# A two-layer encoder trunk on one core: the third part of each feed-forward's down product by seven products, and four last outputs by halves of the tokens

## The chip, the cores and the metric

The kernel runs on one core of one Trainium2 chip. The metric is the device time of one execution in microseconds (us); lower is better. The engines are named as the profile names them: PE is the matrix engine, DVE the vector engine, ACT the scalar engine, POOL and SP the two that issue most DMAs here.

## The reference

512 tokens of width 1024 go through two layers. Each layer is: a SwiGLU feed-forward (inner width 2816), a mixer (layer 0: windowed attention beside a recurrent block; layer 1: gated DeltaNet), a second feed-forward, and a gate that mixes in a per-layer embedding `p`. After the first three parts comes a residual and a layer norm. All is float32.

```python
def swiglu(x, wg, wu, wd):
    return (jax.nn.silu(x @ wg) * (x @ wu)) @ wd

for i in range(DEPTH):
    x = layer_norm(DN_ALPHA * x + 0.5 * swiglu(x, ffn1_wg[i], ffn1_wu[i], ffn1_wd[i]), ln_g[i, 0], ln_b[i, 0])
    y = mixer_ab(x, ...) if i % 2 == 0 else mixer_c(x, ...)
    x = layer_norm(DN_ALPHA * x + y, ln_g[i, 1], ln_b[i, 1])
    x = layer_norm(DN_ALPHA * x + 0.5 * swiglu(x, ffn2_wg[i], ffn2_wu[i], ffn2_wd[i]), ln_g[i, 2], ln_b[i, 2])
    x = x + jax.nn.sigmoid(x @ ple_wg[i] + ple_bg[i]) * (p[i] @ ple_wp[i])
```

## The kernel before, in words

**Layout.** Activations lie feature by token: `xf[0..7]` are eight tiles of 128 features by 512 tokens. A weight tile is 128 by 128. The width 1024 makes `KD = 8` tiles, the inner width 2816 makes `MF = 22` inner tiles.

**Precision.** Every product is done as three matmuls of a shorter float format: a number is split into a high part (a cast on ACT) and a low part (a subtraction on DVE), and `mm3` (line 466) multiplies low by high, high by high and high by low. So each weight tile and each activation tile costs ACT and DVE a cast and a subtraction before PE can use it. The weights' splits are issued by `splitter`, which runs ahead of PE by `self.ahead` steps (`AHEADS = 5` steps inside the feed-forward, `AHEADF = 10` at its end); a step is four weight tiles side by side, 128 by 512, in the plain way.

**Seven products for eight.** `block` multiplies a two by two arrangement (two output tiles by two halves of the tokens, over pairs of input tiles) with seven products in place of eight (`PRODUCTS`). It needs sums and differences of the weights (`s1` to `s4`, made by DVE once and otherwise by DMAs that add in flight, `addload`), differences of the activations (`diffs`, `hforms` for the inner tiles), copies of partial results (`snap`, on ACT) and additions when results are taken out (`done`). Its matmuls are 256 tokens wide.

**A feed-forward** (`ffn`) has the order of `FFN_ORDER`: inner tiles 0 to 6 up, then tiles 0 to 5 down by seven products, tiles 7 to 12 up, tiles 6 to 11 down by seven products, tiles 13 to 21 up, and last tiles 12 to 21 down in the plain way. A `down` block over three pairs of inner tiles has 7 x 3 x 3 = 63 matmuls, there are four of them for eight outputs, and their results are added onto `xf`. Inner tiles that go down by seven products are prepared by `hforms`, the others only split (`self.hs`).

**The feed-forward's end** (`ffn_ln`) does the plain part, output after output over the ten inner tiles that are left, and the layer norm. `first` takes output 0, makes a mean over its features on PE and subtracts it from all eight `xf` (DVE, eight operations 128 by 512). `take` adds an output onto `xf[m]`, squares it (ACT), and adds it and its square onto two running sums (DVE). The last two outputs are done by halves of the tokens: first half of both, then second half of both. When all outputs of a half are taken, `tail` sums over features on PE, makes the norm's factors on DVE and ACT, and spawns eight `apply`, one per feature tile: three DVE and two ACT operations, 128 by 256, that end in the split tile the next stage reads. The next stage starts with a group of four outputs by halves of the tokens (`group(..., halves=True)`): 8 x 12 matmuls of the first half, then as many of the second. After a layer's second feed-forward three small outputs of `p` (`ple_p`, 18 matmuls 512 wide) stand ahead of that group.

**What sets the order.** Each engine executes in the order in which the program issues instructions. The program issues PE's matmuls one after another and weaves the other engines' work between them by times that it estimates (`tick`, `due_at`); on the chip only the order and the waits on data are left. Eight PSUM banks are handed on in turn.

Of the kernel before, what the change touches and what calls it, by code (L numbers as in the profile page):

```python
# [29 lines left out]
KD = D // P  # L30
MF = DFF // P
# [7 lines left out]
HT = T // 2  # L39
TA, TB = slice(0, HT), slice(HT, T)  # L40

FFN_ORDER = (("up", 0, 7), ("down", 0, 6), ("up", 7, 13), ("down", 6, 12), ("up", 13, MF),
             ("plain", 12, MF))
NPLAIN = 3


def stream_plan():


    def ffn():  # L50
        o = [("P", NPLAIN * 2 * KD)]
        for what, a, b in FFN_ORDER:
            if what == "up":
# [169 lines left out]
class Kern:  # L223
# [388 lines left out]
    def y(self, k, cs):  # L612
        self.until(lambda: self.ys[k] is not None)
        return self.ys[k]

    def ffn(self, i, n, l):
# [8 lines left out]
        self.hs = [None] * MF  # L625
        j0 = FFN_ORDER[-1][1]

# [103 lines left out]
        self.ahead = AHEADS  # L731
        for what, a, b in FFN_ORDER:
            if what == "up":
# [9 lines left out]
    def ffn_ln(self, i, l, desc, y, nk):  # L743

        S, V, G, PE = self.S.l, self.V.l, self.G.l, self.PE.l
        self.__dict__.pop("x", None)
        xf = self.xf
        st = {"taken": [0, 0], "c": False}

        def first(p_):  # L750
            yield V.scalar_tensor_tensor(xf[0], p_, 0.5, xf[0], ALU.mult, ALU.add)
            self.psfree(self.V)
            hi, lo = yield from self.split(xf[0])
            pc = yield from self.bank(0)
            yield [PE.matmul(pc, self.ones128, hi.bitcast(F32R), start=True, stop=False),
                   PE.matmul(pc, self.ones128, lo.bitcast(F32R), start=False, stop=True)]
            st["q"], st["s"] = self.tl(), self.tl()
            for m in range(KD):
                yield V.tensor_tensor(xf[m], xf[m], pc, ALU.subtract)
            self.psfree(self.V)  # L760
            yield S.activation(st["q"], xf[0], AF.Square)
            st["c"] = True

        def take(m, p_, cs, free, add):
            while not st["c"]:
                yield None
            yield V.scalar_tensor_tensor(xf[m][:, cs], p_[:, cs], 0.5, xf[m][:, cs], ALU.mult, ALU.add)
            if free:
                self.psfree(self.V)
            sq = self.tl()  # L770
            yield S.activation(sq[:, cs], xf[m][:, cs], AF.Square)
            a, s, q = xf[m][:, cs], st["s"][:, cs], st["q"][:, cs]
            yield add.l.tensor_tensor(s, xf[0][:, cs] if m == 1 else s, a, ALU.add)
            yield add.l.tensor_tensor(q, q, sq[:, cs], ALU.add)
            for half in range(2):
                if cs == FULL or cs == HALVES[half]:
                    st["taken"][half] += 1

        for m in range(KD - 2):
            if m == KD - 4:  # L780
                self.ahead = AHEADF
            p_ = self.mtile(desc(m), y, nk)
            self.spawn(first(p_) if m == 0 else take(m, p_, FULL, True, self.V), 1)
        self.S.activation(self.tiny(1), self.epsln, AF.Abs_reciprocal_sqrt)
        if l != 1:
            self.spawn(self.load_p(i), 2)
        self.xh, self.xl = [None] * KD, [None] * KD
        self.napply = [0, 0]
        ps, ws = {}, {}
        st["p"] = [self.ps() for _ in range(2)]  # L790
        for half, cs in enumerate(HALVES):
            for m in (KD - 2, KD - 1):
                if half == 0:
                    ps[m] = self.ps()
                for k in range(nk):
                    if half == 0:
                        ws[m, k] = self.w(desc(m)(k))
                    yh, yl = y(k, cs)
                    self.mm3(ps[m][:, cs], ws[m, k], yh[:, cs], yl[:, cs], k == 0, k == nk - 1)
                self.spawn(take(m, ps[m], cs, half == 1, self.V), 1)  # L800
            self.spawn(self.tail(i, l, half, cs, st), 1)
        self.ahead = 6
        self.xdone, self.xs = lambda k: self.napply[1] > k, lambda k: (self.xh[k], self.xl[k])
# [910 lines left out]
```

## Time and profile before

| what | value |
|---|---|
| median of 2 runs | 2029.3 us (2028.8 to 2029.8) |
| the profiled execution's own time | 2027.8 us |
| its span in the profile | 2026.1 us |
| mean granted clock of PE | 0.996 |
| PE busy, DVE busy, ACT busy | 98%, 80%, 61% |
| moved by DMA | 273.69 MB, mean 135 GB/s |

The span is what the profile covers; the execution's own time has 1.7 us more around it. A busy PE in the profile is not a PE at its peak, since matmuls overlap, so durations of stretches of matmuls are worked out from the distance between starts. The same holds for DVE and ACT: an operation's length in the timeline overlaps the next one's start, and the distance from start to start is what it takes from the engine.

### The profile page before, as it was taken

How to read it: one execution, taken by the hardware profiler on the slowest of the kernel's cores; microseconds unless marked ns; L12 is line 12 of the kernel's file. 1: busy time of each engine (PE TensorE's matmuls, PEld its weight loads, DVE VectorE, ACT ScalarE, POOL GpSimd, SP SyncE). 2: the span in 40 equal slices, each digit the busy share in tenths (PEclk: the TensorE clock that was granted, in tenths of full speed). 3: DMA queues.
4: the chain of work that ended last, by engine and by line, in shares of the span. 5: the costliest groups of instructions: out<-in, count | busy, mean ns of one | idle time of the engine just before them, and what ended most of it. 6: DMA issues, size and time to landing. Idle time of an engine off the chain costs nothing.

```text
span 2026.1 us, 39662 instructions
## 1 busy us (share of the span) xinstructions
PE 1991.8 (98%) x15237; PEld 1844.4 (91%) x15237; DVE 1621.3 (80%) x3360; ACT 1235.4 (61%) x2841; POOL 322.5 (16%) x372
## 2 busy tenths in 40 slices
PE   8999999999999999999999999999999999999999
PEld 7999998878899999898999998987877989999988
DVE  8888777779998887788888777887776898887676
ACT  5666664796766666465666664685644566666554
POOL 1223210000023232000232210021100013232100
PEclk9999999999999999999999999999999999999999
DMA  7787975123358798424797974131221257888631
GB/s 228 153 195 163 201 170 177 32 64 103 92 122 199 155 208 181 138 82 108 145 205 155 207 172 146 44 101 53 52 80 54 66 122 165 186 178 191 164 102 42
DMA packets 105053, 273.69 MB, mean 135 GB/s; under 512 B 11792, under 2 KB 25248, under 8 KB 104864
## 3 DMA queue, kind: packets, MB, share of 16 engines
q1 hardware_dynamic: 57024, 188.81, 29.8%
q0 software_dynamic: 47840, 82.35, 26.1%
q8 instruction: 120, 1.97, 0.4%
q14 instruction: 69, 0.57, 0.1%
HBM read 269.00 MB, written 2.11 MB: 134 GB/s over the span
## 4 chain that ended last, share of the span: by engine, by line
PE 76%; DVE 16%; ACT 5%; DMA 2%; issue 2%; SPq 0%; POOL 0%; DVEq 0%; ACTq 0%; POOLq 0%
PE ps L162 76%; DVE t L162 15%; ACT t L162 4%; DMA wr<-w 1%; DMA t<-w 1%; ACT L162 0%; SPq L1499 0%; DVE y L162 0%; POOL y L162 0%; POOL t L433 0%; DVEq L162 0%; DVE der L162 0%; ACTq L162 0%; ACT y L162 0%; DVE o L162 0%
## 5 line engine op out<-in xcount | busy, mean ns | idle before, releaser
L162 PE MATMUL ps<-t,t 128*128 128x256 f32 (+4 forms) x14824 | 1964.5, 296 | 30.0 <-DVE t L162 19.9
L162 PEld LDWEIGHTS ps<-t,t 128*128 128x128 f32 (+2 forms) x14824 | 1798.5, 184 | 167.1 <-DVE t L162 40.0
L162 DVE TENSOR_TENSOR t<-t,t 128x512 fp32r<-128x512 f32 (+4 forms) x870 | 477.5, 574 | 89.3 <-ACT t L162 79.4
L162 DVE TENSOR_TENSOR t<-wr,t 128x512 fp32r<-128x512 f32 (+2 forms) x729 | 463.2, 659 | 19.8 <-ACT t L162 13.7
L162 ACT CAST t<-t 128x512 fp32r<-128x512 f32 (+2 forms) x697 | 357.0, 537 | 172.7 <-DVE t L162 159.7
L162 ACT CAST t<-wr 128x512 fp32r<-128x512 f32 (+2 forms) x729 | 402.4, 598 | 2.6 <-DMA wr<-w 2.6
L162 ACT COPY t<-ps 128x256 f32<-128x256 f32 (+1 forms) x475 | 184.1, 389 | 252.6 <-PE ps L162 249.1
L433 POOL DMA_DIRECT2D wr<-w x108 | 93.2, 863 | 1046.0 <-DVE t L162 749.6
L162 DVE SCALAR_TENSOR_TENSOR t<-t,t 128x256 f32<-128x256 f32 (+1 forms) x348 | 177.1, 515 | 75.3 <-ACT t L162 68.4
L433 POOL DMA_DIRECT2D t<-w x216 | 191.3, 1000 | 137.7 <-DVE t L162 51.3
L162 ACT ACTIVATE t<-t 128x256 f32<-128x256 f32 (+1 forms) x190 | 93.6, 500 | 182.7 <-DVE t L162 179.4
L162 DVE SCALAR_TENSOR_TENSOR t<-ps,t 128x256 f32<-128x256 f32 (+2 forms) x174 | 84.5, 489 | 67.2 <-PE ps L162 66.6
L162 DVE TENSOR_TENSOR t<-t 128x256 f32<-128x256 f32 x212 | 89.2, 421 | 57.9 <-ACT t L162 54.5
L162 ACT ACTIVATE t<-ps 128x128 f32<-128x128 f32 (+2 forms) x204 | 70.8, 358 | 88.4 <-PE ps L162 86.9
L162 DVE TENSOR_TENSOR t<-ps,t 128x256 f32<-128x256 f32 (+2 forms) x188 | 81.8, 435 | 13.9 <-PE ps L162 10.1
L162 DVE SCALAR_TENSOR_TENSOR t<-ps,vec,t 128x511 f32<-128x511 f32 (+3 forms) x92 | 68.3, 746 | 20.6 <-ACT t L162 16.4
L162 DVE TENSOR_TENSOR t<-wr,wr 128x512 f32<-128x512 f32 (+1 forms) x108 | 69.6, 644 | 1.9 <-DMA wr<-w 1.9
L162 ACT ACTIVATE t<-t,vec,der 128x256 f32<-128x256 f32 x96 | 56.0, 597 | 4.5 <-DVE t L162 4.5
L162 ACT ACT_TABLE_LOAD x37 | 47.5, 1283 | 11.1 <-DVE t L162 8.5
L162 POOL TENSOR_TENSOR y<-y,sm 128x8 f32<-128x8 f32 (+1 forms) x16 | 22.7, 1420 | 188.2 <-DVE y L162 188.2
L162 DVE SCALAR_TENSOR_TENSOR t<-t,der,t 128x256 f32<-128x256 f32 x96 | 45.7, 477 | 0.0
L162 DVE TENSOR_TENSOR t<-t,ps 128x512 f32<-128x512 f32 (+1 forms) x62 | 33.3, 578 | 7.3 <-PE ps L162 5.6
(69 smaller groups left out, 438.1 us busy)
## 6 DMA issues: line engine op xcount, KB each, us to landing
wr<-w SPq DMA_DIRECT2D x296, 512.0 KB, 4.3
t<-w POOLq DMA_DIRECT2D x152, 256.0 KB, 5.9
wr<-w SPq DMA_DIRECT2D x66, 384.0 KB, 3.6
wr<-w POOLq DMA_DIRECT2D x76, 256.0 KB, 4.8
t<-w POOLq DMA_DIRECT2D x64, 192.0 KB, 4.8
wr<-w POOLq DMA_DIRECT2D x32, 192.0 KB, 4.3
t<-x SPq DMA_DIRECT2D x8, 256.0 KB, 6.1
t<-p SPq DMA_DIRECT2D x8, 256.0 KB, 4.9
```

Of the source, the lines that this page charges most:

```text
L162: getattr(self.e, op.name)(*op.a, **op.kw)
L433: self.nc.gpsimd.dma_start(t, src, accum_op=ALU.add)
```

## The change

Tiles 12 to 17 go down by seven products too, ahead of the last three up tiles; only tiles 18 to 21 go down in the plain way. At the end four outputs, not two, are done by halves of the tokens. `self.ahead` goes to 10 at the first plain output, not at the fifth.

```diff
-FFN_ORDER = (("up", 0, 7), ("down", 0, 6), ("up", 7, 13), ("down", 6, 12), ("up", 13, MF),
-             ("plain", 12, MF))
+FFN_ORDER = (("up", 0, 7), ("down", 0, 6), ("up", 7, 13), ("down", 6, 12), ("up", 13, 19), ("down", 12, 18),
+             ("up", 19, MF), ("plain", 18, MF))
+
+NHALF = 4
...
-        for m in range(KD - 2):
-            if m == KD - 4:
+        for m in range(KD - NHALF):
+            if m == 0:
                 self.ahead = AHEADF
...
-            for m in (KD - 2, KD - 1):
+            for m in range(KD - NHALF, KD):
```

In the whole program PE gets 912 more matmuls 256 wide and 528 fewer 512 wide. DVE gets 244 more operations 256 wide, 128 more 384 wide and 72 fewer 512 wide. POOL issues 48 more DMAs that add in flight.

The first place is DVE at the end of the first feed-forward of layer 0, where the last outputs are taken (`t_80` to `t_87` are `xf[0]` to `xf[7]`, `wr` are raw weights, `ps` are PSUM banks). Before, output 6 and output 7 of the first half:

```order
L162 SCALAR_TENSOR_TENSOR t_86<-ps_4563,t_86 128x256
L162 TENSOR_TENSOR t_4621<-wr_4461,t_4620 128x512
L162 TENSOR_TENSOR t_4300<-t_4300,t_86 128x256
L162 TENSOR_TENSOR t_4299<-t_4299,t_4616 128x256
L162 TENSOR_TENSOR t_4640<-wr_4461,t_4639 128x512
L162 TENSOR_TENSOR t_4570<-t_4567,t_4569 128x512
L162 TENSOR_TENSOR t_4664<-wr_4476,t_4663 128x512
L162 SCALAR_TENSOR_TENSOR t_87<-ps_4613,t_87 128x256
L162 TENSOR_TENSOR t_4300<-t_4300,t_87 128x256
L162 TENSOR_TENSOR t_4299<-t_4299,t_4673 128x256
L162 TENSOR_TENSOR t_4684<-t_4300,t_4684 128x256
```

After, output 3 whole, then outputs 4 to 7 of the first half:

```order
L164 SCALAR_TENSOR_TENSOR t_83<-ps_4829,t_83 128x512
L164 SCALAR_TENSOR_TENSOR t_84<-ps_4853,t_84 128x256
L164 SCALAR_TENSOR_TENSOR t_85<-ps_4875,t_85 128x256
L164 TENSOR_TENSOR t_4808<-t_4808,t_83 128x512
L164 TENSOR_TENSOR t_4807<-t_4807,t_4898 128x512
L164 TENSOR_TENSOR t_4808<-t_4808,t_84 128x256
L164 TENSOR_TENSOR t_4807<-t_4807,t_4905 128x256
L164 TENSOR_TENSOR t_4808<-t_4808,t_85 128x256
L164 TENSOR_TENSOR t_4807<-t_4807,t_4911 128x256
L164 SCALAR_TENSOR_TENSOR t_86<-ps_4891,t_86 128x256
L164 SCALAR_TENSOR_TENSOR t_87<-ps_4908,t_87 128x256
L164 TENSOR_TENSOR t_4808<-t_4808,t_86 128x256
```

The weight splits between the outputs are gone, and four outputs of the first half are taken one behind the other.

The second place is DVE a little later, where the first half is normalised (`der` holds the norm's gains). Before, from output 3's first operation on:

```order
L162 SCALAR_TENSOR_TENSOR t_4774<-t_83,der,t_4710 128x256
L162 TENSOR_TENSOR t_4844<-ps_4562,t_4844 128x256
L162 TENSOR_TENSOR t_4749<-t_82,t_4748 128x256
L162 TENSOR_TENSOR t_83<-t_4774 128x256
L162 SCALAR_TENSOR_TENSOR t_4824<-t_84,der,t_4710 128x256
L162 SCALAR_TENSOR_TENSOR t_4844<-t_4844 128x256
L162 SCALAR_TENSOR_TENSOR t_4845<-t_4844,t_4845 128x256
L162 TENSOR_TENSOR t_4845<-ps_4561,t_4845 128x256
L162 TENSOR_TENSOR t_4776<-t_83,t_4775 128x256
L162 TENSOR_TENSOR t_84<-t_4824 128x256
L162 SCALAR_TENSOR_TENSOR t_4851<-t_85,der,t_4710 128x256
L162 TENSOR_TENSOR t_4826<-t_84,t_4825 128x256
```

After, from output 2's last operation to output 4's first:

```order
L164 TENSOR_TENSOR t_5054<-t_82,t_5053 128x256
L164 TENSOR_TENSOR t_4813<-wr_4669,t_4812 128x512
L164 TENSOR_TENSOR t_5135<-wr_4669,t_5134 128x512
L164 TENSOR_TENSOR t_5142<-wr_4703,t_5141 128x512
L164 TENSOR_TENSOR t_5151<-wr_4703,t_5150 128x512
L164 TENSOR_TENSOR t_5162<-wr_4744,t_5161 128x512
L164 TENSOR_TENSOR t_5166<-wr_4744,t_5165 128x512
L164 TENSOR_TENSOR t_5078<-t_5075,t_5077 128x512
L164 SCALAR_TENSOR_TENSOR t_5063<-t_83,der,t_5010 128x256
L164 TENSOR_TENSOR t_83<-t_5063 128x256
L164 SCALAR_TENSOR_TENSOR t_5106<-t_84,der,t_5010 128x256
```

Six weight splits, and one of `p`, now stand between output 2 and output 3; before, the norm of outputs 3 to 5 ran through with no split between.

## Rows read from the trace of the kernel before

**Rows 1.** The page, part 1: busy time, share of the span, instructions.
```profile
PE 1991.8 (98%) x15237; PEld 1844.4 (91%) x15237; DVE 1621.3 (80%) x3360; ACT 1235.4 (61%) x2841; POOL 322.5 (16%) x372
```

**Rows 2.** Windows of the first feed-forward; columns: window, length, busy (instructions), clock, DMA, GB/s.
```profile
120.00:180.00 60.00, 58.70 (x483) 57.89 (x482) 48.16 (x96) 39.33 (x91) 15.57 (x18) 1.00 0.77 164
180.00:220.00 40.00, 39.90 (x330) 39.42 (x329) 34.40 (x73) 24.21 (x57) 13.04 (x15) 1.00 0.92 205
240.00:300.00 60.00, 60.00 (x502) 60.00 (x501) 42.61 (x75) 37.46 (x83) 11.29 (x13) 1.00 0.78 177
301.00:357.00 56.00, 56.00 (x307) 48.85 (x306) 40.31 (x71) 25.32 (x48) 4.32 (x8) 1.00 0.53 169
```

**Rows 3.** Timeline, DVE, first feed-forward's end; start, length, engine, line, operation, tiles, idle, releaser.
```profile
301.72 0.69 DVE L162 SCALAR_TENSOR_TENSOR t<-t,t 128x512 f32<-128x512 f32 x1 [0.74 <-ACT t L162]
...
303.10 0.69 DVE L162 TENSOR_TENSOR t<-t,t 128x512 fp32r<-128x512 f32 x1
...
311.09 4.87 DVE L162 TENSOR_TENSOR t<-t,ps 128x512 f32<-128x512 f32 x8 [0.28 <-PE ps L162]
...
322.21 0.69 DVE L162 SCALAR_TENSOR_TENSOR t<-ps,t 128x512 f32<-128x512 f32 x1 [2.05 <-PE ps L162]
...
329.01 0.69 DVE L162 SCALAR_TENSOR_TENSOR t<-ps,t 128x512 f32<-128x512 f32 x1 [2.91 <-PE ps L162]
...
350.29 1.77 DVE L162 TENSOR_TENSOR t<-t,t 128x256 f32<-128x256 f32 x4
...
356.80 0.42 DVE L162 TENSOR_TENSOR t<-t 128x256 f32<-128x256 f32 x1
```

**Rows 4.** The same timeline, later: 256-wide operations back to back.
```profile
377.96 0.42 DVE L162 TENSOR_TENSOR t<-t 128x256 f32<-128x256 f32 x1
378.30 0.47 DVE L162 SCALAR_TENSOR_TENSOR t<-t,der,t 128x256 f32<-128x256 f32 x1
```

**Rows 5.** Timeline, DVE, stretch 180 to 220: 384-wide weight splits.
```profile
195.73 1.49 DVE L162 TENSOR_TENSOR t<-wr,t 128x384 fp32r<-128x384 f32 x3
```

**Rows 6.** Timeline, PE, first feed-forward's end.
```profile
357.71 1.95 PE L162 MATMUL ps<-t,t 128*128 128x256 f32 x12 [0.29 <-ACT t L162]
...
360.28 0.39 PE L162 MATMUL ps<-t,o 128*128 128x256 f32 x1 [0.18 <-DVE t L162]
...
365.39 18.98 PE L162 MATMUL ps<-t,t 128*128 128x256 f32 x155 [0.67 <-DVE t L162]
```

**Rows 7.** Timeline, PE, second feed-forward's end.
```profile
874.27 7.56 PE L162 MATMUL ps<-t,t 128*128 128x256 f32 x49
...
883.77 21.51 PE L162 MATMUL ps<-t,t 128*128 128x256 f32 x178
```

**Rows 8.** Timeline, PE, second stretch of inner tiles and what follows.
```profile
122.79 13.21 PE L162 MATMUL ps<-t,t 128*128 128x256 f32 x108 [0.31 <-ACT t L162]
136.35 20.42 PE L162 MATMUL ps<-t,t 128*128 128x256 f32 x168 [0.36 <-DVE t L162]
...
177.82 72.45 PE L162 MATMUL ps<-t,t 128*128 128x256 f32 x595 [0.28 <-DVE t L162]
```

**Rows 9.** Timeline, PE, end of layer 0's mixer.
```profile
539.27 7.58 PE L162 MATMUL ps<-t,t 128*128 128x256 f32 x48 [2.13 <-DVE t L162]
```

**Rows 10.** Windows of 2 us, end of layer 0's mixer.
```profile
540.00:542.00 2.00, 2.00 (x12) 2.00 (x11) 1.84 (x6) 1.50 (x4) 0.00 (x0) 0.51 0.97 242
542.00:544.00 2.00, 2.00 (x14) 2.00 (x13) 1.01 (x3) 0.73 (x2) 0.00 (x0) 0.64 0.90 304
```

**Rows 11.** Timeline, PE, end of layer 1's mixer.
```profile
1632.59 28.29 PE L162 MATMUL ps<-t,t 128*128 128x256 f32 x165 [1.72 <-ACT t L162]
```

**Rows 12.** Windows of 2 us, end of layer 1's mixer.
```profile
1632.00:1634.00 2.00, 1.38 (x4) 1.09 (x5) 1.90 (x6) 1.82 (x4) 0.00 (x0) 0.57 0.68 162
1634.00:1636.00 2.00, 2.00 (x11) 2.00 (x11) 1.58 (x5) 1.02 (x3) 0.00 (x0) 0.50 1.09 320
...
1638.00:1640.00 2.00, 2.00 (x15) 2.00 (x14) 2.00 (x5) 1.30 (x4) 1.71 (x3) 0.72 0.38 44
```

## The prediction

> **What bounds the kernel now.** I read the page's busy shares first, then windows by stage, then the timelines of PE and DVE at the places that the change touches. PE is busy for 98% of the span and its weight loads for 91%, DVE for 80% [rows 1]. The windows show that this 80% is no even load: DVE has 48.2 of 60 us in the second stretch of inner tiles, 34.4 of 40 in the second down part, 42.6 of 60 in the third stretch and 40.3 of 56 in the plain part at the end [rows 2]. So PE sets the pace, and the plain part is where DVE has room: it waits 2 to 3 us for each output [rows 3]. The change takes matmuls away from PE and puts more DVE work next to the one place where PE waits for DVE by construction, the layer norm.
>
> **Paces.** From start to start, a 256-wide matmul takes 0.120 us (502 in 60 us [rows 2]); a 512-wide one 0.227 us (30 matmuls between two outputs taken at 322.21 and 329.01, 6.80 us [rows 3]). DVE takes 0.60 for a 512-wide operation (eight in 4.87, less the overlap of the last [rows 3]), 0.34 for a 256-wide one (377.96 to 378.30 [rows 4]), about 0.40 with the norm's gains, by their length [rows 4], and 0.47 for a 384-wide one [rows 5].
>
> **Term 1, PE's work.** Per feed-forward, before: six outputs whole, 6 x 30 x 0.227 = 40.8 us, and two by halves, 120 x 0.120 = 14.4, together 55.2. After: 252 matmuls of seven products, 30.2; four outputs whole, 48 x 0.227 = 10.9; four by halves, 96 x 0.120 = 11.5; together 52.6. That is -2.6 per feed-forward, -10.3 us for four. The saving is small because a 512-wide matmul costs less than two 256-wide ones: one product in eight is saved, and 6% of that width's speed is given back.
>
> **Term 2, the third part's inner tiles.** Tiles 12 to 17 now need differences and splits of activations, as tiles 6 to 11 do. In that stretch PE waits 0.31, 0.36, 0.36 and 0.28 us, once at the start and once per pair of tiles [rows 8]; in the third stretch it waits for nothing (60.00 of 60 [rows 2]). I take the same 1.3 us for the new pairs: +5.2 us in all. Ends: 0, if the waits fall into slack, and 8. The weights' sums come by 12 more adding DMAs per feed-forward on POOL's queue and by raw tiles of 384 KB on SP's; the second down part runs with the DMA engines 92% busy and PE busy for 39.9 of 40 us [rows 2], so I cost them at nothing. If that cover were gone, a late sum would hold a block, and the term's upper end allows for it.
>
> **Term 3, the end of a feed-forward that a mixer follows (two of four).** Zero is PE's first plain matmul; in the trace of before DVE's last operation for the last inner tile starts 0.5 us behind it, at 301.72. From there to the operation that ends output 0 of the first half, the changed order has 57 DVE rows without a break for PE: 28 that are 512 wide (the splits of the last weights and of four steps of the mixer's, the eight subtractions, four whole outputs), 28 that are 256 wide (four half outputs three times over, two of the second half, the statistics) and one with gains. 28 x 0.60 + 28 x 0.34 + 0.40 = 26.7 us, so the last of them starts at 26.9, and the first product follows 0.9 later (356.80 to 357.71 in before [rows 3, 6]): 27.8. PE's own work to there is 10.9 + 11.5, two 512-wide matmuls for the mean and four 256-wide statistics, 0.9, and 0.4 for the last inner tile's split, which now is wanted at the tenth plain matmul (2.0 us) and not the twenty-eighth: 23.7. So PE waits 4.1 us. Then the eight groups of twelve, 11.5 us plus 0.5 of statistics, are paced by DVE: the next 40 rows (24 that are 256 wide, 9 that are 512 wide, 7 with gains) take 16.4 us, and because six weight splits and one of `p`, 4.2 us, stand between output 2 and output 3, the fourth group can start at about 38.8 and the eighth ends at 46.3. That is 6.5 us more of waiting. Total, with the 0.4, 11.0, against 0.29 + 0.18 + 0.67 = 1.2 in before [rows 6]: +9.8 each, +19.6 us. Ends: +4 each if the splits slip behind the group or DVE overlaps better, +14 each if ACT, which casts for each of these splits, is late too.
>
> **Term 4, the end that a gate follows (the other two).** The same 57 rows stand on DVE, but 18 matmuls of `p`, 4.1 us, stand on PE ahead of the group: 23.7 + 4.1 = 27.8, so the first wait is covered. The first three groups then wait 2.4 us for DVE's statistics of the second half; with the 0.4 above 2.8 us, where before PE ran through [rows 7]. +5.6 us in all; ends 0 and +12, since weight splits stand between the outputs of the second half as well.
>
> **Term 5, PE's clock.** No run here shows PE idle 4 us at this place. The nearest rows are the mixers' ends: after 2.13 us of idling the granted clock is 0.51 and 0.64 of full for 2 us each, 1.7 us lost [rows 9, 10]; after 1.72 us idle it is 0.57, 0.50, 0.50 and 0.72, 3.4 us lost [rows 11, 12], where the window left out reads like the one before it. I take 2.6, the mean, for each mixer-side end: +5.2 us. Ends: 0, if slow groups only fill the wait for DVE, and 5.8 each, half speed for four groups.
>
> **Sum.** -10.3 + 5.2 + 19.6 + 5.6 + 5.2 = +25.3 us. The profiled execution took 2027.8 us (span 2026.1 and 1.7 around it); the median is 1.5 above that. So 2029.3 + 25.3, about 2054 us. With all terms at their low ends it is -10 + 8 = 2027; with all at their high ends, -10 + 8 + 28 + 12 + 12 = +50, 2079. Two per cent of the time before is 40.6 us, about what a measurement of this kernel can tell from no change: 1988.7 and 2069.9 are the bounds, and the forecast is a small loss within them.
>
> **Rivals.** *A, PE stays the only bound.* If the ends of the feed-forwards keep their cover, only terms 1 and, in part, 2 are left: -10.3 to -5, 2019 to 2024, not slower than before. Its place is the norm of the first half, its price the 57 rows; it decides if DVE needs under 23 us for them. For it: DVE is idle 28% of the plain part now [rows 2]. Against it: that part shrinks from 55 to 23 us of PE's work, and the mean's eight subtractions and eight outputs' takings stay. The Trainium skill, Perfetto Trace Analysis, section Identifying the Most-Contended Engine, judges TensorE by its weight-load share and the others by occupancy and has one optimise the highest first; by that rule this change is right, and it would give A's time. The trace agrees with the ranking (91% to 80%) but its windows show that the ranking turns over at the norm, so I give A little.
>
> *B, the clock stays down through the whole group.* The gaps between groups of twelve come again and again, each a chance to lose the clock; at 0.5, the lower of its two levels, eight groups take 23.0 us, not 11.5. Two such ends cost 2 x 11.5 where I took 2 x 2.6: +18, 2072. It decides if the granted clock is 0.5 until the group's second half. For it: the 1.72 us gap cost 6 us of low clock [rows 11, 12]. Against it: groups five to eight come without a gap, and the waits of 0.18 and 0.67 us in before left the clock whole. [...]
>
> **Chances.** The forecast 0.72, with 2036 to 2068 as its own range; A 0.13; B 0.15. The range that is to hold the time eight times in ten leaves out most of A and the far end of B: 2027 to 2076. Slower by over 2%: most of B and a little of the forecast's upper end, 0.12. Faster by over 2% would need 40 us where PE's work shrinks by 10: 0.01. Within 2%: 0.87.
>
> **What would show it.** In the changed profile: PE's busy time down by about 8 to 10 us plus what a low clock adds; PE rows at the first and third feed-forwards' ends with waits for DVE of about 4 us before the first group and 4 before the fourth; waits of 0.3 to 0.4 us per pair of tiles in the third stretch; a granted clock under 1 right behind the first and third feed-forward; DVE near 10 tenths there. It would be wrong if the waits at those ends stay near 1 us (then A), if the clock is low for over 6 us there (then B), or if PE waits for weights in the third down part, which nothing above prices.

## The result and the profile after

The kernel after takes 2091.55 us (median; 2091.33 to 2091.77), before 2029.3. The ratio is 1.0311, with a 95% interval of 1.0294 to 1.0328: 62 us slower, where the forecast was 25 us and its range ended at 2076. The prediction was wrong.

The page of after, part 1, which answers to [rows 1]:

```profile
PE 2009.8 (96%) x15621; PEld 1869.1 (89%) x15621; DVE 1719.6 (82%) x3660; ACT 1293.3 (62%) x3012; POOL 364.4 (17%) x420
```

PE's busy time rose by 18 us although it has less work, and its share fell by two points: the granted clock was 0.982 over the span, not 0.996, and PE waited more. The view of waits says for whom (us in total, times, longest). Before:

```profile
PE ps L162 <- DVE t L162: 20.3, 38, 3.7
PE ps L162 <- ACT t L162: 9.3, 10, 4.2
```

After:

```profile
PE ps L164 <- ACT t L164: 44.1, 21, 4.6
PE ps L164 <- DVE t L164: 31.4, 65, 3.4
```

The sum goes from 29.6 to 75.5 us. Where these waits stand is seen by marks. Each layer norm makes a mean over the features by a pair of 512-wide matmuls with the tile of ones, `ps<-t,o`, and these rows cut the PE timeline into stages (first feed-forward and mixer of layer 0, then of layer 1). Before:

```profile
310.43 0.62 PE L162 MATMUL ps<-t,o 128*128 128x512 f32 x2
...
493.53 0.62 PE L162 MATMUL ps<-t,o 128*128 128x512 f32 x2
...
1226.16 0.62 PE L162 MATMUL ps<-t,o 128*128 128x512 f32 x2
...
1586.37 0.62 PE L162 MATMUL ps<-t,o 128*128 128x512 f32 x2
```

After:

```profile
339.77 0.62 PE L164 MATMUL ps<-t,o 128*128 128x512 f32 x2
...
505.84 0.62 PE L164 MATMUL ps<-t,o 128*128 128x512 f32 x2
...
1281.07 0.62 PE L164 MATMUL ps<-t,o 128*128 128x512 f32 x2
...
1637.04 0.64 PE L164 MATMUL ps<-t,o 128*128 128x512 f32 x2
```

The first difference, 29.3 us, is the third part, which now stands ahead of the mean; the same 29.3 is taken from the stage that ends at 1281.07 and given to the next one, so that each place holds one whole feed-forward. For each other kernel below, its own first difference is used. So, in us over before:

| kernel | first feed-forward, layer 0 | second, layer 0 | first of layer 1, with its mixer | second, layer 1 | span |
|---|---|---|---|---|---|
| predicted | +11.1 | +1.5 | +11.1 | +1.5 | +25 |
| after | +12.3 | +13.3 | +25.1 | +12.8 | +63.5 |
| tiles only | +9.3 | +18.3 | +25.2 | +15.5 | +68.3 |
| halves only | -2.5 | +1.1 | +14.0 | +0.6 | +13.2 |
| banks | +11.2 | +14.8 | +13.2 | +15.0 | +54.1 |
| p, first try | +11.0 | +13.3 | +25.1 | +10.5 | +59.8 |
| p up | +8.4 | +7.7 | +23.7 | +7.2 | +47.1 |
| no mean | +2.4 | +8.9 | +18.4 | +6.6 | +36.2 |
| banks, p, look-ahead | +10.2 | +6.4 | +10.1 | +11.2 | +37.9 |
| the same, no mean | +3.3 | +1.0 | +4.1 | +2.2 | +10.6 |
| halves, all reliefs, no mean | -1.5 | +5.7 | +1.9 | +3.1 | +9.2 |
| halves and banks | -3.0 | +0.3 | -0.9 | +0.7 | -2.9 |
| before, no mean | -2.1 | +3.0 | -2.0 | +0.6 | -0.5 |

Each row is one execution. The last one, of a kernel that takes as long as before, shows how far the places move by themselves: up to 3 us, so smaller differences are not read here.

The first column came near the forecast. The second and fourth missed by some 12 us each, and the third by 14, of which layer 0's column says that about 13 lie in the mixer. These three places are the 37 us that the forecast lacked.

**The first feed-forward's end** has the waits that the prediction walked to. PE's timeline there, against [rows 6]:

```profile
361.74 2.43 PE L164 MATMUL ps<-t,t 128*128 128x256 f32 x9 [4.37 <-ACT t L164]
...
374.53 20.70 PE L164 MATMUL ps<-t,t 128*128 128x256 f32 x146 [3.13 <-ACT t L164]
```

There is a wait of 4.37 ahead of the first group and one of 3.13 ahead of the fourth. ACT is named because it casts last, but the view of DVE shows who is late, against [rows 3]:

```profile
340.49 4.87 DVE L164 TENSOR_TENSOR t<-t,ps 128x512 f32<-128x512 f32 x8
345.27 1.29 DVE L164 SCALAR_TENSOR_TENSOR t<-ps,t 128x512 f32<-128x512 f32 x2
...
368.81 3.69 DVE L164 TENSOR_TENSOR t<-wr,t 128x512 fp32r<-128x512 f32 x6
372.43 0.68 DVE L164 TENSOR_TENSOR t<-t,t 128x512 fp32r<-128x512 f32 x1
```

The idle of 2 to 3 us ahead of each output is gone: the outputs are ready before DVE is. The six weight splits and the one of `p` stand where the order of instructions had them, and the fourth group waits behind them. Windows of 2 us there (columns as in [rows 2]):

```profile
368.00:370.00 2.00, 2.00 (x11) 2.00 (x11) 1.97 (x5) 2.00 (x5) 0.00 (x0) 0.50 0.00 0
...
376.00:378.00 2.00, 2.00 (x11) 2.00 (x11) 1.90 (x7) 1.98 (x5) 0.00 (x0) 0.50 0.13 51
...
380.00:382.00 2.00, 2.00 (x16) 2.00 (x16) 1.82 (x6) 1.23 (x4) 0.00 (x0) 0.82 0.00 0
382.00:384.00 2.00, 2.00 (x19) 2.00 (x18) 1.90 (x6) 1.65 (x4) 0.00 (x0) 1.00 0.04 8
```

The clock is 0.50, the lower of its two levels (1.2 and 2.4 GHz), behind each of the two waits, with 11 matmuls per window and not 19, and it is whole again from about 381 on.

**The second feed-forward's end**, where [rows 7] show no wait at all:

```profile
895.78 0.39 PE L164 MATMUL ps<-t,o 128*128 128x256 f32 x1 [4.57 <-ACT t L164]
896.35 0.58 PE L164 MATMUL ps<-t,o 128*128 128x256 f32 x1 [0.18 <-DVE t L164]
...
902.84 32.53 PE L164 MATMUL ps<-t,t 128*128 128x512 f32 x225 [4.58 <-ACT t L164]
```

That is 9.3 us of waiting where 2.8 was forecast. What waits is told by the order of PE's instructions there (`t2298` and `t2299` are high and low part of `p`'s first tile, `t2332` and `t2333` of its second, `t2330` and `t2334` the second half's running sums, `o2` the ones):

```
L164 MATMUL ps2315_11919<-t2298_11761,t2273_11670 128x512
L164 MATMUL ps2315_11919<-t2298_11761,t2272_11669 128x512
L164 MATMUL ps2294_11755<-t2330_11952,o2_116 128x256 [waits Activation_49]
L164 MATMUL ps2294_11755<-t2330_11952,o2_116 128x256 [waits DVE_49]
L164 MATMUL ps2315_11919<-t2299_11762,t2272_11669 128x512 [waits DVE_49]
L164 MATMUL ps2295_11756<-t2334_11966,o2_116 128x256 [waits Activation_49]
L164 MATMUL ps2295_11756<-t2334_11966,o2_116 128x256 [waits DVE_49]
L164 MATMUL ps2315_11919<-t2332_11958,t2273_11670 128x512 [waits Activation_49]
```

After two matmuls of `p` PE stands at the second half's statistics, which DVE adds up only between the norm's operations of the first half (4.57 us), and then at the second tile of `p`, whose cast and subtraction stand behind the casts of four normalised tiles (4.58). The other 15 matmuls of `p` queue behind both. Both loads of `p` are issued long before, at 874.4 and 874.9, and by the profile take about 5 us to land, so it is the place of the splits on ACT and DVE and not the load that is late. The clock falls here too; from 896 to 906 the windows show 0.50 to 0.53:

```profile
904.00:906.00 2.00, 2.00 (x6) 1.57 (x6) 1.54 (x5) 1.38 (x3) 0.00 (x0) 0.50 0.00 0
```

**The end of layer 1's mixer** has no instruction that the change touches. Before, the serial chains of heads 6 and 7 (DeltaNet steps, 128 wide, each waiting on the last) ran at the same time; now they run one after the other, and PE waits for the end of the second:

```profile
1628.03 1.12 PE L164 MATMUL ps<-cst,t 128*128 128x128 f32 x4 [3.38 <-DVE t L164]
```

The end of each chain is seen on POOL, which takes the power of its norm. Before, the two lie 4 us apart:

```profile
1567.84 1.01 POOL L162 TENSOR_TENSOR y<-y,sm 128x4 f32<-128x4 f32 x1 [44.46 <-DVE y L162]
1572.02 1.01 POOL L162 TENSOR_TENSOR y<-y,sm 128x4 f32<-128x4 f32 x1 [3.17 <-DVE y L162]
```

and after 17:

```profile
1609.36 1.36 POOL L164 TENSOR_TENSOR y<-y,sm 128x4 f32<-128x4 f32 x1 [38.01 <-DVE y L164]
1626.05 1.01 POOL L164 TENSOR_TENSOR y<-y,sm 128x4 f32<-128x4 f32 x1 [15.33 <-DVE y L164]
```

### The profile page after: what moved, and what is told of

It is laid out like the page before. It is cut to its first block, busy times and chain, and to the rows that moved or that the text cites. A ratio compares the mean times of both kernels' runs of the same rounds, so it can differ in the third digit from the quotient of the medians.

```text
span 2089.6 us, 41202 instructions
## 1 busy us (share of the span) xinstructions
PE 2009.8 (96%) x15621; PEld 1869.1 (89%) x15621; DVE 1719.6 (82%) x3660; ACT 1293.3 (62%) x3012; POOL 364.4 (17%) x420
## 3 DMA queue, kind: packets, MB, share of 16 engines
q0 software_dynamic: 54752, 91.79, 27.8%
## 5 line engine op out<-in xcount | busy, mean ns | idle before, releaser
L164 PE MATMUL ps<-t,t 128*128 128x256 f32 (+3 forms) x15208 | 1978.1, 294 | 62.5 <-ACT t L164 34.7
L164 PEld LDWEIGHTS ps<-t,t 128*128 128x128 f32 (+1 forms) x15208 | 1821.6, 185 | 191.1 <-DVE t L164 54.3
L164 DVE TENSOR_TENSOR t<-t,t 128x512 fp32r<-128x512 f32 (+4 forms) x982 | 517.8, 560 | 90.3 <-ACT t L164 81.3
L164 ACT CAST t<-t 128x512 fp32r<-128x512 f32 (+2 forms) x781 | 393.2, 530 | 170.4 <-DVE t L164 160.2
L164 ACT COPY t<-ps 128x256 f32<-128x256 f32 (+1 forms) x539 | 208.3, 388 | 294.0 <-PE ps L164 289.3
L435 POOL DMA_DIRECT2D wr<-w x124 | 107.0, 863 | 1103.9 <-DVE t L164 744.6
L164 DVE SCALAR_TENSOR_TENSOR t<-t,t 128x256 f32<-128x256 f32 (+2 forms) x436 | 213.6, 497 | 80.2 <-ACT t L164 70.0
L435 POOL DMA_DIRECT2D t<-w x248 | 219.5, 987 | 166.3 <-DVE t L164 54.1
L164 DVE SCALAR_TENSOR_TENSOR t<-ps,t 128x256 f32<-128x256 f32 (+2 forms) x230 | 104.3, 464 | 19.1 <-PE ps L164 19.1
L164 DVE SCALAR_TENSOR_TENSOR t<-ps,vec,t 128x511 f32<-128x511 f32 (+3 forms) x92 | 68.3, 747 | 18.5 <-ACT t L164 14.6
L164 DVE TENSOR_TENSOR t<-wr,wr 128x512 f32<-128x512 f32 (+1 forms) x124 | 78.6, 634 | 0.7 <-DMA wr<-w 0.7
L164 DVE TENSOR_TENSOR t<-t,ps 128x512 f32<-128x512 f32 (+1 forms) x62 | 33.3, 580 | 11.1 <-PE ps L164 9.5
```

Of the source, the lines that this page charges most:

```text
L164: getattr(self.e, op.name)(*op.a, **op.kw)
L435: self.nc.gpsimd.dma_start(t, src, accum_op=ALU.add)
```

## The experiments

**One part alone: the tiles, the halves.** The third part by seven products with two last outputs by halves as before:

```diff
-NHALF = 4
+NHALF = 2
...
-            if m == 0:
+            if m == KD - 4:
```

> The change without its second half: the third part goes down by seven products, but two last outputs are done by halves as before, and the look-ahead goes up at the fifth output. Theory (the loss is made where feed-forwards end and in layer 1's mixer, not by the seven products): PE has 2 x 24 x 0.12 = 5.8 us of halves to cover the norm and not 11.5, and DVE takes five whole outputs first, so each end is as bad or worse than in the changed kernel; in layer 1's mixer head 7's chain stands behind head 6's, as in the changed kernel. 2085 to 2105 us. Rival (the four outputs by halves are what costs): 2025 to 2045.

Measured: 2094.32 us, ratio 1.0328 (1.0311 to 1.0345). And the old order of the feed-forward with four outputs by halves:

```diff
-FFN_ORDER = (("up", 0, 7), ("down", 0, 6), ("up", 7, 13), ("down", 6, 12), ("up", 13, 19), ("down", 12, 18),
-             ("up", 19, MF), ("plain", 18, MF))
+FFN_ORDER = (("up", 0, 7), ("down", 0, 6), ("up", 7, 13), ("down", 6, 12), ("up", 13, MF),
+             ("plain", 12, MF))
```

> Only four outputs by halves, with the ten inner tiles plain as before. Theory: the ends have 28.8 us of halves on PE, so the wait of 1.2 us there goes away and 0.8 us of matmul time per feed-forward comes on: within 3 us of before but for layer 1's mixer, where this order too puts head 7's chain behind head 6's: +10 to +14. So 2038 to 2047, and all of the gain over before sits in layer 1's mixer. Rival (halves cost by themselves): over 2050, spread over the four ends. Rival (the mixer's order is no matter): 2027 to 2033.

Measured: 2040.35 us, ratio 1.0062 (1.0047 to 1.0077). Both are as expected: the loss at the feed-forwards' ends comes with the tiles alone (2094.32 us against 2091.55 with the halves, with intervals that overlap), and the halves alone lose in layer 1's mixer and nowhere else (+14.0 in the table). The tiles alone lose there as well, and the ends of the two chains lie 17 to 18 us apart on POOL in both kernels (1611.32 and 1629.12, 1571.15 and 1588.00). The two losses in the mixer don't add: it is one trap that either part springs.

**The mixer's trap.** The program lets a head take a PSUM bank only while more than two are free (`bank(keep=2)`). The layer norm's group of four outputs holds four banks from its start. The suspicion: in the changed order that group starts before the last two heads ask, and head 7 gets its two banks only when head 6 gives its own up. The edit lets these two heads take the last banks:

```diff
-        po = yield from self.bank()
-        pw = yield from self.bank()
+        po = yield from self.bank(0 if h >= 6 else 2)
+        pw = yield from self.bank(0 if h >= 6 else 2)
```

> The changed kernel, but heads 6 and 7 of layer 1's mixer may take the last two PSUM banks, so head 7's chain need not stand behind head 6's. Theory (of the loss 12 to 13 us come from the two chains standing one behind the other for want of a bank): 2076 to 2082 us, the stretch between the first feed-forward's mean and the mixer's mean in layer 1 shorter by 10 to 13 us. Rival (PE waits there for another reason, such as weights or DVE load): no change, 2089 to 2093.

Measured: 2080.95 us, ratio 1.0261 (1.0246 to 1.0277). From mean to mean that mixer took 344.5 us where after took 356.0 (1637.04 - 1281.07). POOL's view of this kernel:

```profile
1611.00 1.01 POOL L164 TENSOR_TENSOR y<-y,sm 128x4 f32<-128x4 f32 x1 [38.85 <-DVE y L164]
1616.33 1.01 POOL L164 TENSOR_TENSOR y<-y,sm 128x4 f32<-128x4 f32 x1 [4.32 <-DVE y L164]
```

The chains overlap again. 11.5 us come from the banks alone, of the 13 that the place lost. So the want of banks is shown as the cause; that the group's start had moved ahead of the two heads stays a suspicion, since the order there was not looked at.

**`p` earlier, a first try.** Its load is spawned ahead of the first plain output:

```diff
+        if l != 1:
+            self.spawn(self.load_p(i), 2)
         for m in range(KD - NHALF):
...
         self.S.activation(self.tiny(1), self.epsln, AF.Abs_reciprocal_sqrt)
-        if l != 1:
-            self.spawn(self.load_p(i), 2)
```

> The changed kernel, but the loads and splits of p are issued ahead of the first plain output, not behind the last whole one. Theory (at the second feed-forwards' ends PE's 18 matmuls of p, which should cover the norm, stand behind the second half's statistics and wait for p's own split): the two waits of 4.6 us there shrink to under 2 us together, with the clock that goes with them: 8 to 12 us less at each of the two ends, in all 2068 to 2077 us. Rival (DVE's norm chain alone sets the end there): no more than 2 us less, 2087 to 2092.

Measured: 2087.22 us, ratio 1.0295 (1.028 to 1.0311): a miss. `load_p` issues the second tile's load only when the first tile's split is out. In the trace both loads and both casts do come earlier (the second tile's cast at 876.06 and not 902.18), but the second tile's subtraction on DVE moved only from 903.01 to 894.56 and still stands among the norm's operations. PE waited 3.96 us for it at the same place.

**`p` earlier, both tiles**, loaded together and split ahead of the last three up tiles:

```diff
             if what == "up":
+                if b == MF:
+                    self.spawn(self.load_p(i), 2)
...
+        ts = [self.tl() for _ in range(2)]
         for k in range(2):
-            t = self.tl()
-            self.nc.sync.dma_start(t, self.a["p"][i, k])
-            self.landing(t, 6.0)
-            self.p[k] = yield from self.split(t)
+            self.nc.sync.dma_start(ts[k], self.a["p"][i, k])
+            self.landing(ts[k], 6.0)
+        for k in range(2):
+            self.p[k] = yield from self.split(ts[k])
```

> The changed kernel, with both loads of p issued one behind the other, and split, before the last three up tiles. Theory (the norm's cover at a second feed-forward's end is lost because PE's products of p wait for the second tile of p, whose split stands behind the norm's work): the two waits of 4.6 us there become under 1.5 us together, 8 to 12 us less at each of the two ends; the first feed-forwards' ends and the mixer keep their loss: 2065 to 2075 us. Rival (DVE's norm chain sets the end, p or no p): 2083 to 2091.

Measured: 2075.98 us, ratio 1.0238 (1.0217 to 1.0258). PE's timeline at the second feed-forward's end:

```profile
891.30 1.67 PE L164 MATMUL ps<-t,t 128*128 128x256 f32 x9 [0.27 <-ACT t L164]
...
896.29 0.38 PE L164 MATMUL ps<-t,o 128*128 128x256 f32 x1 [2.50 <-DVE t L164]
897.07 38.26 PE L164 MATMUL ps<-t,t 128*128 128x256 f32 x243 [0.39 <-ACT t L164]
```

That is 3.2 us of waiting in place of 9.3; each second feed-forward gains 5.6, the first ones 4 and 1. The waits were expected to fall under 1.5 us together and the gain to be 8 to 12 at each, so the cause is confirmed and its size is not. With `p` on time PE has something to do through the first wait, and what is left is the statistics of the second half.

**Less for DVE: no mean.** After without the eight subtractions of the mean:

```diff
             for m in range(KD):
-                yield V.tensor_tensor(xf[m], xf[m], pc, ALU.subtract)
+                pass
```

> The changed kernel without the eight subtractions of the mean over output 0's features at each feed-forward's end (that shift is left out; the norm takes off the whole mean itself). Theory (DVE's rows between the plain products and the first product after set the ends): eight operations of 0.60, 4.8 us, go from that chain, so the first wait of 4.4 to 4.6 us shrinks to under 1 us at each of the four ends and the low clock behind it goes at least in part: 4 to 7 us less at each, 2062 to 2076 us. Rival (ACT, which the releaser column names, or PE's order sets the first wait): waits stay over 3 us, 2083 to 2091.

Measured: 2063.6 us, ratio 1.0175 (1.0151 to 1.0199). Its PE timeline at the first feed-forward's end:

```profile
358.58 3.07 PE L164 MATMUL ps<-t,t 128*128 128x256 f32 x12 [3.05 <-ACT t L164]
...
364.97 0.50 PE L164 MATMUL ps<-t,t 128*128 128x256 f32 x2 [0.78 <-ACT t L164]
366.39 20.64 PE L164 MATMUL ps<-t,t 128*128 128x256 f32 x168 [0.92 <-DVE t L164]
```

The total is as expected, the way isn't: the first wait fell by only 1.3 us, the second by 2.2 of its 3.1. The first wait is what PE can't cover of a fixed stretch: from the start of the first half's last statistics on PE to the first product it is 4.9 us in before, in after and here alike (352.83 to 357.71, 356.86 to 361.74, 353.70 to 358.58), filled by norm factors and the first tile's split. What differs is the plain work that PE still has to do behind these statistics: 35 matmuls in before, one in after, 12 here. The second wait fell for another reason too. The program's estimates moved with the edit, and weight splits went with them: here eight stand between the outputs, from 336.09 to 347.48, where after has six behind output 2, at 368.81. So the gain of 28 us is that of the eight operations (4.87 us of DVE at each end) together with the order that they force on the splits; the two were not parted. The same edit on the kernel before is the control:

```diff
 # the kernel before
             for m in range(KD):
-                yield V.tensor_tensor(xf[m], xf[m], pc, ALU.subtract)
+                pass
```

> The kernel before without the mean's eight subtractions (the shift of the tokens before the squares is not made). Theory: in before the plain part covers them, since PE waits only 0.29 us ahead of the first half's group, so leaving them out changes nothing: 2025 to 2030. Rival: the subtractions cost the path in before too (eight times 0.6 us at four ends): 2008 to 2015. Where the same edit took 28 us off the changed kernel, the difference is what the change made of that cover.

Measured: 2028.28 us, ratio 1.0002 (0.9993 to 1.0011). The same instructions, with what they push behind them, cost 28 us in the changed kernel and nothing in before: DVE's work at a feed-forward's end lay under the long plain part, and the change took the cover away.

**All reliefs together.** After with the banks, `p` as above, and the look-ahead raised at the last up tiles:

```diff
                 if b == MF:
                     self.spawn(self.load_p(i), 2)
+                    self.ahead = AHEADF
```

> The changed kernel with the two banks for heads 6 and 7, with p split before the last three up tiles, and with the look-ahead raised to 10 there too, so that weight splits leave the norm's chain. Theory (three causes that add: first feed-forwards' ends, second ones, the mixer): the mixer gives back 11 us, the second feed-forwards' ends 16 to 24, the look-ahead 3 to 4 us at each first end: 2045 to 2060 us. Rival (the causes are one, and overlap): over 2065.

Measured: 2062.29 us, ratio 1.0164 (1.0148 to 1.018), a little above what was expected; the gains of banks and of `p` add (10.6 + 15.6 of the 29.3). Then also without the mean's subtractions:

> As the kernel before this one of the list (banks, p early, look-ahead early), and without the eight subtractions of the mean at the four ends. Theory: all three causes and the longest piece of DVE's chain are gone, what is left is PE's saving of 10 us less 5 us of waits in the third part and a few us at the ends: 2025 to 2042 us. Rival (the seven products of the third part cost DVE more than they save, spread over the feed-forward): over 2045.

Measured: 2040.69 us, ratio 1.0057 (1.0042 to 1.0072). At the first feed-forward's end PE still waits 3.30 and 0.67 us.

**What is the third part worth by itself?** The same kernel with the old order of the feed-forward, so that only the third part is undone:

```diff
-FFN_ORDER = (("up", 0, 7), ("down", 0, 6), ("up", 7, 13), ("down", 6, 12), ("up", 13, 19), ("down", 12, 18),
-             ("up", 19, MF), ("plain", 18, MF))
+FFN_ORDER = (("up", 0, 7), ("down", 0, 6), ("up", 7, 13), ("down", 6, 12), ("up", 13, MF),
+             ("plain", 12, MF))
```

> The old order of the feed-forward, four outputs by halves, the banks free for heads 6 and 7, p loaded and split ahead of the last up tiles, the look-ahead raised there, and the mean's eight subtractions left out (the shift of the tokens before the squares is not made). Against the run with the same edits and the third part by seven products, which took 2040.7 us, this tells what the third part alone is worth when its ends are relieved. Theory: it is worth nothing or a loss, since its 10 us on PE are given back in waits of its stretch and of the plain part that is too short to cover the norm: 2020 to 2030 here. Rival: the third part does bring its 10 us and the rest of the loss is in the halves: then 2040 to 2052 here.

Measured: 2037.07 us, ratio 1.0044 (1.0031 to 1.0056). The third part shows no gain against this (the intervals of 1.0057 and 1.0044 overlap), as the theory had it. But the time is 7 us above the theory's range and 3 under the rival's: with a long plain part the reliefs themselves cost (it is 2027.48 us below with the banks alone), so the pair is no clean price of the third part. PE's timeline ahead of the second feed-forward's end, and ACT's behind its releaser, show a piece of this:

```profile
754.62 36.25 PE L164 MATMUL ps<-t,t 128*128 128x256 f32 x300 [1.39 <-ACT t L164]
...
753.67 0.62 ACT L164 CAST t<-t 128x512 fp32r<-128x512 f32 x1 [1.52 <-DMA t<-w]
```

The cast that PE waits for had itself waited 1.52 us for weights that a DMA was still bringing. Why they come late with the look-ahead raised, and where the rest of the 7 us lies, was not looked for.

**The better half of the change.** Old order, four outputs by halves, and the banks:

```diff
-FFN_ORDER = (("up", 0, 7), ("down", 0, 6), ("up", 7, 13), ("down", 6, 12), ("up", 13, 19), ("down", 12, 18),
-             ("up", 19, MF), ("plain", 18, MF))
+FFN_ORDER = (("up", 0, 7), ("down", 0, 6), ("up", 7, 13), ("down", 6, 12), ("up", 13, MF),
+             ("plain", 12, MF))
...
-        po = yield from self.bank()
-        pw = yield from self.bank()
+        po = yield from self.bank(0 if h >= 6 else 2)
+        pw = yield from self.bank(0 if h >= 6 else 2)
```

> The old order of the feed-forward (only tiles 0 to 11 by seven products), four outputs by halves, and heads 6 and 7 of layer 1's mixer free to take the last PSUM banks. Theory: halves alone took 2040.4 us, and its whole loss sat in layer 1's mixer (374.4 us from mean to mean against 360.2 of before), because the four outputs' group holds four banks while head 7 waits for two. With the banks free the mixer comes back to 360 to 363, and the time to 2026 to 2031, no different from before. Rival: the loss in that mixer is the walk of four outputs by halves itself, and no bank: then 2037 to 2041 as without the edit.

Measured: 2027.48 us, ratio 0.9994 (0.9985 to 1.0003), no different from before. At the first feed-forward's end the waits of [rows 6] are gone, all three:

```profile
362.32 19.34 PE L164 MATMUL ps<-t,t 128*128 128x256 f32 x158
```

What is gained there (1.2 us of waits at each first feed-forward) is too little to stand out over the run. No version beat the kernel before.

## Why the prediction was wrong, step by step

**Term 1**, PE's work, -10.3: not seen as a gain anywhere. With all reliefs PE's busy time was 1992.1 us with the third part and 1995.3 without, 3 us less, at a clock of 0.995 against 0.997, and the time was 3.6 us more. The sign was right; the size can't be read from these runs, and waits and the clock eat what there is.

**Term 2**, waits of the third part's inner tiles, 1.3 per feed-forward: about right. PE's timeline of after, against [rows 8]:

```profile
228.98 20.41 PE L164 MATMUL ps<-t,t 128*128 128x256 f32 x168 [0.36 <-DVE t L164]
...
270.44 65.55 PE L164 MATMUL ps<-t,t 128*128 128x256 f32 x527 [0.27 <-DVE t L164]
332.83 3.16 PE L164 MATMUL ps<-t,t 128*128 128x256 f32 x13
336.24 3.69 PE L164 MATMUL ps<-t,t 128*128 128x512 f32 x15 [0.25 <-DVE t L164]
```

The waits are 0.36 twice and 0.27, together 0.99 in the stretch, and the last row is the 0.4 (measured 0.25) for the last inner tile's split. It stands at the twelfth plain matmul and not at the tenth. The weights' sums cost next to nothing, as taken: PE waits for no weight here, and 0.48 us in layer 0's second feed-forward, for a cast that a weight sum held up.

**Term 3**, the end that a mixer follows: right in its mechanism, too large in its size. Zero, the first plain matmul, is at 333.07: the row that starts at 332.83 is the end of the one above it, from a view that begins at 333, and of its 13 matmuls the first two are 256 wide and still belong to the inner tiles. The walk had the first group start at 27.8, which is 360.9 (measured 361.74), after a wait of 4.1 (4.37), and the fourth group at 38.8, 371.9 (374.53, with the low clock between). All waits of this end together were 8.3 us (4.37, 0.19, 0.33, 3.13 and the 0.25), not 11.0.

**Term 5**, the clock there, 2.6: too small. PE worked for some 14.4 us at half speed (361.74 to about 370.4 less 0.5 of waits, and 374.53 to about 380.7), which costs 7.2 us, an estimate from the rows and windows above. Part of this filled waits that term 3 had counted, as the term's low end had considered: waits and clock together were 15.5 where the two terms have 13.6. So the place came out near, +12.3 where +11.1 was forecast, partly by luck, since two sizes were wrong in opposite directions. By the prediction's own sign, a clock that is low for over 6 us, rival B came: it was low from 360 to about 370 and from 374 to 381. By its price B did not come: 11.5 us at each such end was for a clock that stays at 0.50 until the group's second half, and here about a third of the first half's 96 matmuls ran at full speed again. The Trainium skill, TensorE: Matmul & The Clock Gate, section HAM oscillation, describes a kernel whose bursts of matmuls, with waits of about 3 to 5 us between them, each restart at half rate. The trace agrees with that for the waits of 4.37 and 3.13 us; the waits of 0.78 and 0.92 us in the kernel without the mean are shorter than the section's, and there the clock stayed at 1.00:

```profile
358.00:360.00 2.00, 1.42 (x6) 1.36 (x7) 2.00 (x7) 1.49 (x5) 0.00 (x0) 0.60 0.00 0
...
364.00:366.00 2.00, 0.70 (x4) 0.30 (x2) 1.93 (x6) 1.88 (x5) 0.00 (x0) 1.00 0.00 0
366.00:368.00 2.00, 1.61 (x13) 1.61 (x14) 2.00 (x8) 1.29 (x4) 0.00 (x0) 1.00 0.00 0
```

**Term 4**, the end that a gate follows, failed. The step was that "18 matmuls of `p`, 4.1 us, stand on PE ahead of the group" and cover the first wait. They stand ahead of the group, but behind two things that are late themselves: the second half's statistics and the second tile of `p`. The cover stood in the queue behind the waits that it was to cover. 2.8 us of waits were forecast, 9.3 were measured, and the clock, for which no term was taken here, fell to 0.50 as well: PE is busy for 5.2 us in the windows from 896 to 906, so some 2.6 us went there (an estimate). The place took +13 where +1.5 was forecast. The experiment with `p` on time gave back 5.6 of it each, and the one without the mean 4 to 6; together with the look-ahead and the banks they bring it to +1.0 and +2.2.

**A place without a term.** The mixer of layer 1 was costed at nothing, because the change has no instruction there. But all order in this program comes from estimated times, so a change in one stage moves the weave in a later one; there two heads came to want banks that were held, for 11.5 of the place's 13 us, as the edit of the banks shows. Both this and term 4 could be read ahead of the run: PE's order at the second feed-forward's end, and the place of the last heads' steps in the order of layer 1's mixer, are as fixed as the piece of DVE's order that the walk of term 3 was made from.

The rivals: A was wrong, since DVE needed more than PE's work at each end. The rule cited for it, that of the engine with the highest share, picked PE, and with less work on PE the time rose by 3.1%. The same page of the Trainium skill, Perfetto Trace Analysis, section Optimization Strategy, says that in some kernels the most-contended engine changes over time, and speaks of optimizing within each such regime. The traces agree with that: PE is the busiest engine of the whole span, and 28 us hang on DVE's eight operations, and on the order behind them, at four ends.

## What to carry to other kernels

Before work is taken off the busiest engine, ask what that work covers: here a plain part of 55 us hid a layer norm, and 23 us could not. A cover counts only if its instructions can start when the wait begins, so read the order on the waiting engine and the data that each of them needs. Where a program weaves its order by estimates and hands out a pool of buffers, look at the whole order again, not only at the edited stage: a loss can come up a mixer later.

## What the runs showed of the hardware

The length of a wait alone does not tell whether the clock falls. Behind waits of PE of 3.05, 3.13, 4.37 and 4.58 us it was at 0.5 to 0.6, and with waits of 0.78 and 0.92 it stayed at 1.00. Between these the same wait went both ways: 2.13 us at the end of layer 0's mixer was followed by 0.51 and 0.64 in before [rows 9, 10], and 2.15 us at the same place by 1.00 in the kernel with `p` up. So a price for the clock that is taken from one or two such rows, as in term 5, is a rough one.

```profile
547.75 4.95 PE L164 MATMUL ps<-t,t 128*128 128x256 f32 x36 [2.15 <-DVE t L164]
...
548.00:550.00 2.00, 2.00 (x15) 1.72 (x15) 1.87 (x6) 1.02 (x3) 0.00 (x0) 1.00 0.65 187
```
